# One class for the eight PSUM banks, shared SBUF buffers, and new orders for two stages of a two-layer decoder step

## The chip, the core and the metric

The kernel runs on one core of a Trainium2 chip, as one program. The metric is the device time of one execution in microseconds (us), lower is better. A core has five engines that each work through a list of instructions of their own, in order: TensorE (PE, matrix products; its weight loads are shown apart as PEld), VectorE (DVE), ScalarE (ACT), GpSimd (POOL), and SyncE (SP, which here only issues DMA transfers). Products are written to PSUM, which this kernel cuts into eight banks of 128 x 512 numbers; operands lie in SBUF.

## The reference, cut to what matters

One step of a two-layer decoder for a prompt of 512 tokens and 8 samples of one token each, so 520 columns. Layer 0 is sparse attention with a paged cache, layer 1 is an mLSTM with four heads of width 512.

```python
for i in range(DEPTH):                       # 2 layers, D_MODEL 1024
    hp = rmsnorm(yp, norm_w[i]);  hs = rmsnorm(ys, norm_w[i])
    if i % 2 == 0:
        dp, kvp, wp = nsa_prompt(hp, *prm)
        ds, kvs, wsm = nsa_sample(hs, cache_kv[l], cache_win[l], page_table, *prm)
    else:
        dp, Cp, np_, mp, cp = mlstm_mixer(hp, ...)      # prompt, from a zero state
        ds, Cs, ns_, ms, cs = mlstm_mixer(hs, state_conv[l], state_C[l], state_n[l], state_m[l], ...)
    yp = yp + dp;  ys = ys + ds
y_prompt = rmsnorm(yp, final_norm_w);  y_sample = rmsnorm(ys, final_norm_w)

def nsa_attend(...):          # three branches, each a masked softmax, mixed by gates
    ...
    return gates[..., 0:1] * o_c + gates[..., 1:2] * o_s + gates[..., 2:3] * o_w

def mlstm_mixer(h, conv_buf, C0, n0, m0, chunk, ...):
    proj = h @ w_in;  xm, z = proj[..., :D_INNER], proj[..., D_INNER:]     # D_INNER 2048
    ...                                      # conv of width 4, silu, q, k, v in blocks of 4, gates
    hc, C, n, m = mlstm_cell(...)            # S, num / max(|den|, .), new C and n
    hn = hc * lax.rsqrt(jnp.mean(hc * hc, axis=-1, keepdims=True) + RMS_EPS)
    out = (hn * norm_w + skip * c) * jax.nn.silu(z)
    return out @ w_out, C, n, m, xpad[:, T:]
```

## The kernel before, in words

**Tiling.** Everything is kept transposed: 128 features on the partitions, the 520 tokens along the free axis, in two halves of 260 where a projection is made. A weight is loaded as float32 (`wraw`), rounded to a high part (`whi`, on ACT or DVE) and a low part (`wlo` = raw - hi, on POOL or DVE), and each product is three matmuls, hi by hi, lo by hi, hi by lo. The activations are split in the same way (`hhi`/`hlo` after the norms, `uh`/`ul` before the output projection). A result leaves PSUM on DVE or ACT: `x<-x,mm`, for instance, is DVE adding a finished product to the residual, and it is the last reader of that bank.

**Stages.** `step_kernel` runs through them in this order: (1) norm, k and v projections, and the compression of the cache pages of the samples (0 to about 205 us); (2) the q and z projections (to about 300); (3) attention, prompt tiles and samples interleaved (about 300 to 470); (4) the output projection of layer 0, the `xm` projection and the convolution of layer 1 (to about 650); (5) the z projection with the first states of the samples (to about 757); (6) the heads alone: q, k, v, the scores, the other states and the output projection of the heads that are done (to about 1009); (7) the rest of the output projection, the final norm and the last rows of C.

**What sets the order.** The program is recorded, and then each engine's list is emitted in an order that is written down: five stages as a list of swaps (`MOVED...`), and three as a permutation of the pieces of a plan: `ORDER0` for attention, `ORDER1` for stage 5, `ORDER2` for stage 6, with `MOVEDP0` to `MOVEDP2` naming the pieces that run on another engine than the plan's own. No engine overtakes within its list, so an instruction that waits holds up all that stands behind it.

**PSUM.** `bank(tag, bufs, name)` makes a PSUM tile of one bank. The eight banks form four classes: `mm` with 2 (`mmb()`: projections, values, products with the state), `s` with 3 (`sb()`: scores and sums), `t` with 2 (`xb()`: transposes, short rows, `kwh` products), `d` with 1 (`db()`: the samples' scores and products with the state). A new tile of a class takes the place of the oldest one of that class, and its first matmul waits until the last reader of that older tile is done.

**SBUF.** Buffers form rings by tag in the same way: raw, high and low weights 2 each, `w1h` and `w1l` 3 each, the page splits `phi`/`plo` 2 each, the attention's scores 7 (`SBUFS`) and transposed scores 8 (`PTB`), and one ring for each row of the heads (`wb`, `ctw`, `q`, `kwh`, `kwl`, `cpt`; `wt`, `acc`, `sq1`, `hx`, `hy`).

**Names used later.** `dec_qk` (L1163) makes the scores of the samples against one cache tile `dk` (`d<-dk,QZ`, 8 pages loaded by SP), `d<-dk,dpt` is the product with the values. `s<-KA,qst` and `s<-KB,qst` are the prompt's scores, `s<-cst,s` and `t<-cst,s` its transposes, `mm<-pt,VN` its values. In the heads `s<-q,CT` is the score, `hx`, `hy`, `num` are the rows of a head's normalised output, `ul<-num,uh` and `ul<-HN,uh` the low parts of what goes into the output projection (`mm<-uh,whi`), `cs<-t,wk,cs` a state's update. All instructions go through one helper, so a profile shows nearly all of them at line 504; they are told apart by the names of their tiles.

Of the kernel before, what the change touches and what calls it, by code (L numbers as in the profile page):

```python
# [9 lines left out]
F32 = mybir.dt.float32  # L10
F32R = mybir.dt.float32r
# [33 lines left out]
SBUFS = 7  # L45
PTB = 8
# [7 lines left out]
W3B = (2, 6, 6)  # L54
# [486 lines left out]
def step_kernel(ctx, tc, ap):  # L541
# [19 lines left out]
    def bank(tag, bufs, name=None):  # L561
        return ps.tile([128, 512], F32, name=name or tag, tag=tag, bufs=bufs)
# [6 lines left out]
    def mmb():  # L569
        return bank("mm", 2)  # L570

    def sb():
        return bank("s", 3)

    def xb():
        return bank("t", 2)

    def db():
        return bank("d", 1)
# [2286 lines left out]
```

## Time and profile before

| what | value |
|---|---|
| median of 3 runs | 1055.37 us (1055.33 to 1056.41) |
| the profiled execution | 1052.93 us, of which the span of the core is 1051.2 us |
| busy in that span | PE 1022.5, PEld 909.5, DVE 787.8, ACT 535.0, POOL 393.3 us |
| granted TensorE clock, mean | 0.995 |
| read and written | 145.89 MB and 58.10 MB |

The profiled execution is 2.44 us, or 0.23%, below the median of the runs. The span is the time from the first to the last instruction; 1.7 us of the profiled time lie around it. Busy time of PE is counted from the start of a matmul to its modelled end. Matmuls overlap: one of 260 columns lasts 0.28 us in the trace and the next starts 0.12 us later, so that a start that comes up to 0.16 us late leaves no idle time behind.

### The profile page before, as it was taken

The page shows a single profiled execution, that of the slowest core. Times are in us where ns is not written, and L with a number is a line of the kernel's source. Part 1 is how long each engine was busy: PE and PEld are TensorE (multiplying, and loading weights), DVE is VectorE, ACT ScalarE, POOL GpSimd, SP SyncE. Part 2 cuts the span into 40 slices and gives each one's busy share as a digit, 9 for nine tenths or more (in the row PEclk, how much of TensorE's full clock was granted, in tenths as well). Part 3 has the DMA queues.
Part 4 walks back from the last instruction along what each step waited for, and adds up shares of the span by engine and source line. Part 5 has one row for each costly group of instructions (what it writes and reads, how often), then busy time and mean ns, then how long its engine had stood idle before and what let it go on. Part 6 is the DMA issues. An engine that isn't in the chain of part 4 may idle for free.

```text
span 1051.2 us, 24005 instructions
## 1 busy us (share of the span) xinstructions
PE 1022.5 (97%) x8743; PEld 909.5 (87%) x8743; DVE 787.8 (75%) x1877; ACT 535.0 (51%) x1230; POOL 393.3 (37%) x430
## 2 busy tenths in 40 slices
PE   7999999999999999999999999999899999999998
PEld 6989999899988877779999998898867688787897
DVE  6877764478468887876877675886477998988875
ACT  5253332532467786651444364566555555563533
POOL 1162333434324546462324442342423234434332
PEclk9999999999999999999999999999999999999999
DMA  7664554123435524547435652787789879889543
GB/s 248 202 192 141 156 155 131 36 96 121 144 106 177 141 81 130 153 142 251 142 111 163 203 162 73 243 302 275 259 277 328 273 267 303 295 293 325 161 134 112
DMA packets 124792, 197.19 MB, mean 188 GB/s; under 512 B 16117, under 2 KB 66166, under 8 KB 124418
## 3 DMA queue, kind: packets, MB, share of 16 engines
q1 hardware_dynamic: 118866, 186.37, 54.8%
q10 hardware_dynamic: 5808, 9.28, 2.5%
q8 instruction: 69, 1.13, 0.5%
q14 instruction: 49, 0.40, 0.1%
HBM read 145.89 MB, written 58.10 MB: 194 GB/s over the span
## 4 chain that ended last, share of the span: by engine, by line
PE 83%; DVE 8%; ACT 3%; issue 2%; DMA 1%; SPq 1%; POOL 0%; DVEq 0%; ACTq 0%; POOLq 0%
PE mm L504 51%; PE s L504 18%; PE t L504 10%; PE d L504 5%; ACT s L504 1%; DVE num L504 1%; DVE s L504 1%; DVE cs L504 1%; SPq L504 1%; DMA dk<-in_cache 1%; DVE x L504 1%; DVE qst L504 1%; DMA nw<-in_norms 1%; DVE wlo L504 0%; ACT pt L504 0%
## 5 line engine op out<-in xcount | busy, mean ns | idle before, releaser
L504 PE MATMUL mm<-hhi,whi 128*128 128x260 f32 (+1 forms) x952 | 273.9, 288 | 2.2 <-DVE xm L504 1.3
L504 PE MATMUL mm<-hhi,wlo 128*128 128x260 f32 (+1 forms) x952 | 270.4, 284 | 1.0 <-POOL wlo L504 0.7
L504 PE MATMUL mm<-hlo,whi 128*128 128x260 f32 (+1 forms) x952 | 270.3, 284 | 0.0
L504 PEld LDWEIGHTS mm<-hhi,whi 128*128 128x128 f32 (+1 forms) x952 | 179.2, 188 | 7.2 <-issue 1.7
L504 PEld LDWEIGHTS mm<-hhi,wlo 128*128 128x128 f32 (+1 forms) x952 | 179.1, 188 | 1.6 <-POOL wlo L504 0.9
L504 PEld LDWEIGHTS mm<-hlo,whi 128*128 128x128 f32 (+1 forms) x952 | 178.9, 188 | 0.8 <-DVE hlo L504 0.3
L504 POOL TENSOR_TENSOR wlo<-wraw,whi 128x1024 fp32r<-128x1024 f32 (+2 forms) x55 | 108.8, 1979 | 159.0 <-DVE whi L504 74.8
L504 DVE SCALAR_TENSOR_TENSOR cs<-t,wk,cs 128x512 f32<-128x512 f32 x128 | 88.6, 742 | 6.0 <-ACT cs L504 3.8
L504 ACT ACTIVATE cs<-cs,SBC 128x1024 f32<-128x1024 f32 x64 | 72.0, 1142 | 13.2 <-PE d L504 12.5
L504 POOL TENSOR_SCALAR s<-s,sm 128x128 f32<-128x128 f32 (+3 forms) x63 | 62.8, 1008 | 41.8 <-DVE sm L504 21.1
L504 ACT ACTIVATE s<-s,mn 128x256 f32<-128x256 f32 (+3 forms) x128 | 70.6, 554 | 14.7 <-DVE mn L504 12.7
L504 PE MATMUL s<-phi,w1h 128*128 128x256 f32 (+1 forms) x256 | 77.0, 301 | 0.0
L504 PE MATMUL s<-plo,w1h 128*128 128x256 f32 (+1 forms) x256 | 74.5, 291 | 2.2 <-DVE plo L504 2.0
L504 PE MATMUL s<-phi,w1l 128*128 128x256 f32 (+1 forms) x256 | 74.0, 289 | 0.0
L504 ACT ACTIVATE whi<-wraw 128x1024 fp32r<-128x1024 f32 (+1 forms) x55 | 48.0, 874 | 45.2 <-PE mm L504 34.6
L504 PE MATMUL mm<-uh,whi 128*128 128x260 f32 x224 | 66.5, 297 | 3.6 <-DVE x L504 3.6
L504 DVE CUSTOM_DVE_ANT_0 s<-s,D 128x256 f32<-128x256 f32 (+3 forms) x128 | 57.7, 486 | 10.4 <-PE s L504 7.7
L504 PE MATMUL mm<-uh,wlo 128*128 128x260 f32 x224 | 63.3, 282 | 0.0
L504 PE MATMUL mm<-ul,whi 128*128 128x260 f32 x224 | 63.2, 282 | 0.0
L504 DVE TENSOR_TENSOR wlo<-wraw,whi 128x1024 fp32r<-128x1024 f32 (+1 forms) x47 | 51.9, 1106 | 3.1 <-ACT whi L504 1.8
L504 PEld LDWEIGHTS s<-plo,w1h 128*128 128x128 f32 x256 | 48.5, 189 | 3.9 <-DVE plo L504 2.5
L504 PEld LDWEIGHTS mm<-uh,whi 128*128 128x128 f32 x224 | 42.2, 188 | 9.2 <-DVE x L504 4.5
(479 smaller groups left out, 2650.2 us busy)
## 6 DMA issues: line engine op xcount, KB each, us to landing
cs<-in_state_C SPq DMA_DIRECT2D x64, 512.0 KB, 6.0
o_cs<-cs SPq DMA_DIRECT2D x64, 512.0 KB, 4.8
praw<-in_cache SPq DMA_DIRECT2D x128, 128.0 KB, 3.3
dk<-in_cache SPq DMA_DIRECT2D x128, 128.0 KB, 2.9
wraw<-in_m_in SPq DMA_DIRECT2D x32, 512.0 KB, 4.2
wraw<-in_m_out SPq DMA_DIRECT2D x32, 256.0 KB, 4.4
wraw<-in_w_kv SPq DMA_DIRECT2D x11, 512.0 KB, 4.7
wraw<-in_w_q SPq DMA_DIRECT2D x8, 512.0 KB, 3.6
```

Of the source, the lines that this page charges most:

```text
L504: return f(*[real(x) for x in a], **{n: real(x) for n, x in k.items()})
```

## The change: what it does

1. **One PSUM class.** `bank(name)` takes no class and no number; all tiles have the tag `bank` with 8 buffers. `mmb`, `sb`, `xb` and `db` only differ in the name that the tile gets. In the program as built, a new tile then takes the bank that was given back longest ago in 643 of 663 cases.
2. **Score bank kept per tile.** `dec_qk` kept its bank under `D["dst"]`. It now keeps it under `D["dst", u]`, so that a second tile's product may be started before the first has been read.
3. **Shared SBUF rings.** Raw, high and low weights share one ring of 6, the two halves of `w1` one of 6, `phi` and `plo` one of 4, scores and transposed scores one of 15, `cva` and `cvs` one of 4, the block diagonals one of 7, the rows of the heads one of 9 and one of 6; in stages 6 and 7 the `m_out` weights have one of 6, and at the very end one of 20 with `kwh`, `kwl` and `cpt` (`W3B`). No ring is smaller in sum than its parts were.
4. **Orders stated anew.** `ORDER0` with `MOVEDP0` (attention) and `ORDER2` with `MOVEDP2` (heads alone) are other permutations and other choices of engine. `MOVEDP0` names 121 pieces instead of 131 (72 in both), `MOVEDP2` 106 instead of 100 (47 in both). `ORDER1`, `MOVEDP1` and the `MOVED` lists of the other stages stay, and with them the order of PE in those stages.

```diff
-W3B = (2, 6, 6)
+W3B = (8, 6, 6)
 ORDER0 = (
-    792, 8, 13, 28, 9, 11, 14, 10, 31, 16, 15, 29, 17, 54, 830, 0, 12, 32, 914, 18, 37, 33, 34, 55, 911, 19, 59,
...
+    792, 8, 13, 71, 9, 54, 14, 10, 137, 11, 28, 15, 16, 34, 12, 55, 59, 80, 17, 828, 56, 793, 18, 801, 29, 23,
...
-    def bank(tag, bufs, name=None):
-        return ps.tile([128, 512], F32, name=name or tag, tag=tag, bufs=bufs)
+    def bank(name):
+        return ps.tile([128, 512], F32, name=name, tag="bank", bufs=8)
...
-        return bank("mm", 2)
+        return bank("mm")
...
-        return bank("d", 1)
+        return bank("d")
...
-            D["dst"] = db()
+            D["dst", u] = db()
...
-            V.tensor_add(PS[:, u * 128:(u + 1) * 128], PS[:, u * 128:(u + 1) * 128], D["dst"][:, 0:128])
+            V.tensor_add(PS[:, u * 128:(u + 1) * 128], PS[:, u * 128:(u + 1) * 128], D["dst", u][:, 0:128])
...
-            X["raw"] = wp.tile([128, 8, 128], F32, name="wraw", tag="wraw", bufs=WRAW)
+            X["raw"] = wp.tile([128, 8, 128], F32, name="wraw", tag="w", bufs=WRAW + 4)
...
-            X["hi"] = wp.tile([128, 8, 128], F32R, name="whi", tag="whi", bufs=2)
+            X["hi"] = wp.tile([128, 8, 128], F32R, name="whi", tag="w", bufs=WRAW + 4)
...
-            X["lo"] = wp.tile([128, 8, 128], F32R, name="wlo", tag="wlo", bufs=2)
+            X["lo"] = wp.tile([128, 8, 128], F32R, name="wlo", tag="w", bufs=WRAW + 4)
...
-                X["pt", gk] = at.tile([128, 512], F32, name="pt", tag="pt", bufs=PTB)
+                X["pt", gk] = at.tile([128, 512], F32, name="pt", tag="sp", bufs=SBUFS + PTB)
...
-            X["kwh"] = c2.tile([128, T], F32R, name="kwh", tag="kwh", bufs=1)
+            X["kwh"] = c2.tile([128, T], F32R, name="kwh", tag="row", bufs=9)
...
-            X["x"] = ce.tile([128, T], F32, name="hx", tag="hx")
+            X["x"] = ce.tile([128, T], F32, name="hx", tag="row", bufs=6)
...
-        pk, kh = xb(), fn.tile([128, T], F32R, name="kwh", tag="kwh", bufs=2)
+        pk, kh = xb(), fn.tile([128, T], F32R, name="kwh", tag="w", bufs=20)
```

The built program shows what the new orders move. Three places follow; line numbers in the kernel after are one lower than before.

**SP, early in attention.** `dk<-in_cache` is the load of one of eight pages of a cache tile, `ISA` ahead of it sets its address, `TENSOR_LOAD pt` reads the page numbers of the next tile, and `wraw<-in_w_o` are weights of the output projection, which stage 4 uses. Before, between two of the first tiles of attention (at 312.93 us in the trace):

```order
L504 ISA
L504 DMA dk<-in_cache 128x256
L504 DMA wraw<-in_w_o 128x1024 x2
L777 TENSOR_LOAD pt
L777 ISA x16
L504 ISA
```

and after:

```order
L503 ISA
L503 DMA dk<-in_cache 128x256
L776 TENSOR_LOAD pt
L776 ISA x16
L503 ISA
```

The two weight loads have moved behind later tiles, one by one tile and the other by three.

**PE, at the third and fourth `d<-dk,QZ` of attention.** Before:

```order
L504 MATMUL s<-KB,qst 128x512
L504 MATMUL d<-dk,QZ 32x128 x16
L504 MATMUL s<-KA,qst 128x384
L504 MATMUL s<-KB,qst 128x384
L504 MATMUL s<-cst,s 128x128 x4
L504 MATMUL t<-cst,s 128x128 x4
L504 MATMUL s<-KA,qst 128x384
L504 MATMUL s<-KB,qst 128x384
L504 MATMUL d<-dk,QZ 32x128 x16
```

and after:

```order
L503 MATMUL s<-KB,qst 128x384
L503 MATMUL d<-dk,QZ 32x128 x16
L503 MATMUL s<-KA,qst 128x512
L503 MATMUL s<-KB,qst 128x512
L503 MATMUL s<-KA,qst 128x512
L503 MATMUL s<-KB,qst 128x512
L503 MATMUL s<-KA,qst 128x384
L503 MATMUL s<-KB,qst 128x384
L503 MATMUL t<-KQ,qst 128x64 x8
L503 MATMUL d<-dk,QZ 32x128 x16
```

The transposes `s<-cst,s` and `t<-cst,s` of the first prompt tile now come after the second of these products, with more scores ahead of them.

**DVE, where the third head is finished.** From the products of `hx` to the last `num` rows, before:

```order
L504 TENSOR_TENSOR hx<-hx,hy 128x512 x2
L504 SCALAR_TENSOR_TENSOR hy<-hx,hy 128x512
L504 TENSOR_TENSOR x_13658<-x_13658,mm 128x260
L504 TENSOR_TENSOR x_12742<-x_12742,mm 128x260
L504 TENSOR_TENSOR num<-num,hy 128x512
L504 SCALAR_TENSOR_TENSOR num<-CT_10968,par,num 128x512
L504 TENSOR_TENSOR num<-num,zs 128x512
L504 TENSOR_TENSOR num<-num,hy 128x512
L504 SCALAR_TENSOR_TENSOR num<-CT_10863,par,num 128x512
L504 TENSOR_TENSOR x_12742<-x_12742,mm 128x260
L504 TENSOR_TENSOR x_12729<-x_12729,mm 128x260
L504 TENSOR_TENSOR num<-num,hy 128x512
```

and after:

```order
L503 TENSOR_TENSOR hx<-hx,hy 128x512 x2
L503 SCALAR_TENSOR_TENSOR hy<-hx,hy 128x512
L503 TENSOR_TENSOR wlo<-wraw,whi 128x512
L503 TENSOR_TENSOR num<-num,hy 128x512
L503 SCALAR_TENSOR_TENSOR num<-CT_10968,par,num 128x512
L503 TENSOR_TENSOR num<-num,hy 128x512
L503 SCALAR_TENSOR_TENSOR num<-CT_10863,par,num 128x512
L503 TENSOR_TENSOR num<-num,zs 128x512
L503 TENSOR_TENSOR x_13513<-x_13513,mm 128x260
L503 TENSOR_TENSOR x_13436<-x_13436,mm 128x260 x2
L503 TENSOR_TENSOR num<-num,hy 128x512
```

From the first of these rows to the last `ul<-HN,uh` of the head DVE now has 8 of the additions to `x` instead of 11, the others standing behind, and one `num<-num,zs` more, which POOL did before. In stages 6 and 7 together DVE has four more `wlo`, four more `whi`, three more `num<-num,zs`, and two more each of `ul<-num,uh` and `acc<-acc,sq`; it has three `q` rows and two `cpt` rows less. In attention the shares of the engines stay within 1 us of what they were, by the durations of the trace of before.

More of the change, by code (lines that the diff above doesn't have):

```diff
@@ L615, in load_w @@
         pool, n = pool or wp, bufs or (WRAW, 2, 2)
-        raw = pool.tile([128, kt, f], F32, name="wraw", tag="wraw", bufs=n[0])
+        raw = pool.tile([128, kt, f], F32, name="wraw", tag="w", bufs=sum(n))
         d = q.dma_start(raw, src)
@@ L619, in load_w @@
             last["w"] = d.ins
-        hi = pool.tile([128, kt, f], F32R, name="whi", tag="whi", bufs=n[1])
+        hi = pool.tile([128, kt, f], F32R, name="whi", tag="w", bufs=sum(n))
         S.activation(hi, raw, AF.Copy)
-        lo = pool.tile([128, kt, f], F32R, name="wlo", tag="wlo", bufs=n[2])
+        lo = pool.tile([128, kt, f], F32R, name="wlo", tag="w", bufs=sum(n))
         lo_of(lo, raw, hi, eng)
@@ L708, in step_kernel @@
     xc, wkv = [], {}
-    raw0 = wp.tile([128, 8, 128], F32, name="wraw", tag="wraw", bufs=WRAW)
+    raw0 = wp.tile([128, 8, 128], F32, name="wraw", tag="w", bufs=WRAW + 4)
     for c in range(2):
@@ L719, in step_kernel @@
     S.preload_act_table_set("natural_log_exp_and_others")
-    hi0 = wp.tile([128, 8, 128], F32R, name="whi", tag="whi", bufs=2)
-    lo0 = wp.tile([128, 8, 128], F32R, name="wlo", tag="wlo", bufs=2)
+    hi0 = wp.tile([128, 8, 128], F32R, name="whi", tag="w", bufs=WRAW + 4)
+    lo0 = wp.tile([128, 8, 128], F32R, name="wlo", tag="w", bufs=WRAW + 4)
     for k in range(2):
@@ L1816, in xm_silu @@
         a, ct = conv.pop(ft), CT[ft]
[L1817 removed]
+        s = mi.tile([128, NTOK], F32, name="cvs", tag="cv", bufs=4)
         sigmoid_into(s, a)
@@ L2143, in load @@
         def load():
-            X["raw"] = wp.tile([128, 8, 128], F32, name="wraw", tag="wraw", bufs=WRAW)
+            X["raw"] = wp.tile([128, 8, 128], F32, name="wraw", tag="w", bufs=WRAW + 4)
             SP.dma_start(X["raw"], ap["m_in"][16 + ft])
         def high():
-            X["hi"] = wp.tile([128, 8, 128], F32R, name="whi", tag="whi", bufs=2)
+            X["hi"] = wp.tile([128, 8, 128], F32R, name="whi", tag="w", bufs=WRAW + 4)
             S.activation(X["hi"], X["raw"], AF.Copy)
         def low():
-            X["lo"] = wp.tile([128, 8, 128], F32R, name="wlo", tag="wlo", bufs=2)
+            X["lo"] = wp.tile([128, 8, 128], F32R, name="wlo", tag="w", bufs=WRAW + 4)
             lo_of(X["lo"], X["raw"], X["hi"], E[e])
@@ L2360, in f_bdk @@
         def f_bdk():
-            X["bdk"] = block_diag(c2, wc[:, 1, ft], "bdk", 5)
+            X["bdk"] = block_diag(c2, wc[:, 1, ft], "bdk", 7, "bd")
         def f_bdm():
-            X["bdm"] = block_diag(c2, mw[:, ft], "bdm", 2)
+            X["bdm"] = block_diag(c2, mw[:, ft], "bdm", 7, "bd")
         def f_ctw():
-            X["ctw"] = big("ctw", n=T) if late else c2.tile([128, T], F32, name="ctw", tag="ctw")
+            X["ctw"] = big("ctw", n=T) if late else c2.tile([128, T], F32, name="ctw", tag="row", bufs=9)
             V.tensor_tensor_reduce(X["ctw"], ct, D["wb_", hd], 1.0, 0.0, op0=OP.mult, op1=OP.add,
@@ L2375, in f_q @@
         def f_q():
-            X["q"] = c2.tile([128, T], F32, name="q", tag="q")
+            X["q"] = c2.tile([128, T], F32, name="q", tag="row", bufs=9)
             S.activation(X["q"], X["po"], AF.Copy)
@@ L2407, in f_cpt @@
         def f_cpt():
-            X["cpt"] = c2.tile([128, T], F32, name="cpt", tag="cpt", bufs=2)
+            X["cpt"] = c2.tile([128, T], F32, name="cpt", tag="row", bufs=9)
             S.activation(X["cpt"], X["pc"], AF.Copy)
@@ L2553, in f_y1 @@
         def f_y1():
-            X["y"] = ce.tile([128, T], F32, name="hy", tag="hy")
+            X["y"] = ce.tile([128, T], F32, name="hy", tag="row", bufs=6)
             S.activation(X["y"], X["x"], AF.Ln)
@@ L2645, in load @@
         def load():
-            X["raw"] = fw.tile([128, 4, 128], F32, name="wraw", tag="wraw", bufs=FWB[0])
+            X["raw"] = fw.tile([128, 4, 128], F32, name="wraw", tag="w", bufs=sum(FWB))
             SP.dma_start(X["raw"], ap["m_out"][ft][:, 4 * hd:4 * hd + 4])
         def high():
-            X["hi"] = fw.tile([128, 4, 128], F32R, name="whi", tag="whi", bufs=FWB[1])
+            X["hi"] = fw.tile([128, 4, 128], F32R, name="whi", tag="w", bufs=sum(FWB))
             S.activation(X["hi"], X["raw"], AF.Copy)
         def low():
-            X["lo"] = fw.tile([128, 4, 128], F32R, name="wlo", tag="wlo", bufs=FWB[2])
+            X["lo"] = fw.tile([128, 4, 128], F32R, name="wlo", tag="w", bufs=sum(FWB))
             lo_of(X["lo"], X["raw"], X["hi"], E[e])
@@ L2752, in step_kernel @@
             mm3(pc, kh[:, s_], kl[:, s_], D["vh_", hd, i], D["vl_", hd, i], i == 0, i == 3)
-        cpt = fn.tile([128, T], F32, name="cpt", tag="cpt", bufs=2)
+        cpt = fn.tile([128, T], F32, name="cpt", tag="w", bufs=20)
         S.activation(cpt, pc, AF.Copy)
```

41 lines of the change are left out of this document (20 added, 21 removed), and 191 rows, old and new, of tables (MOVEDP0, MOVEDP2, ORDER0, ORDER2).

## The prediction

> **What bounds the kernel now.** I read the page first, for the engine that is full, then the windows by stage, for where that engine is not, then its waits and, row by row, its timeline. The page's busy times, two rows of its slices and its chain:
>
> ```profile
> PE 1022.5 (97%) x8743; PEld 909.5 (87%) x8743; DVE 787.8 (75%) x1877; ACT 535.0 (51%) x1230; POOL 393.3 (37%) x430
> PE   7999999999999999999999999999899999999998
> DVE  6877764478468887876877675886477998988875
> PE 83%; DVE 8%; ACT 3%; issue 2%; DMA 1%; SPq 1%; POOL 0%; DVEq 0%; ACTq 0%; POOLq 0%
> ```
>
> PE is the bound: 1022.5 of 1051.2 us, and the change removes no matmul. All that it can win is in the other 28.7 us and in starts that come late under a modelled end. The windows by stage say where (time, then busy us of each engine with its instructions, the clock, DMA share, GB/s):
>
> ```profile
> 0.00:200.00 200.00, 191.35 (x1472) 186.79 (x1473) 135.66 (x268) 80.60 (x198) 68.56 (x71) 1.00 0.52 162
> 200.00:300.00 100.00, 97.22 (x869) 94.88 (x872) 66.21 (x147) 40.10 (x94) 32.57 (x26) 0.98 0.34 105
> 300.00:475.00 175.00, 171.83 (x2020) 140.29 (x2013) 140.42 (x537) 125.25 (x387) 90.69 (x103) 1.00 0.47 139
> 475.00:757.00 282.00, 279.63 (x2380) 265.24 (x2381) 200.40 (x389) 138.47 (x292) 100.27 (x120) 0.99 0.59 199
> 757.00:985.00 228.00, 223.68 (x1601) 167.95 (x1591) 196.06 (x424) 128.28 (x211) 81.33 (x90) 0.99 0.85 286
> 985.00:1012.00 27.00, 24.24 (x198) 22.86 (x198) 25.78 (x64) 9.32 (x21) 8.19 (x7) 1.00 0.57 179
> 1012.00:1051.20 39.20, 34.58 (x242) 31.52 (x240) 23.26 (x52) 12.94 (x30) 11.68 (x13) 1.00 0.32 102
> ```
>
> PE's idle time is 8.65, 2.78, 3.17, 2.37, 4.32, 2.76 and 4.62 us from the first row to the last. In the heads (757 to 1012) DVE is the second full engine, 86% and then 95%. What PE waits for, the rows that matter here:
>
> ```profile
> PE s L504 <- ACT sq L504: 5.6, 1, 5.6
> PE mm L504 <- DVE x L504: 3.6, 4, 1.5
> PE t L504 <- DVE pr L504: 2.4, 1, 2.4
> PE d L504 <- DMA dk<-in_cache: 1.5, 3, 0.8
> PE mm L504 <- DVE xm L504: 1.3, 1, 1.3
> PE t L504 <- ACT cpt L504: 0.7, 1, 0.7
> ```
>
> `mm<-DVE x`, `mm<-DVE xm` and `t<-ACT cpt` have an odd look: a projection reads neither `x` nor `xm`, and the next `cpt` product reads no `cpt`. These are waits for a bank, until the engine that empties it has finished. The timeline shows them (start, length, and in brackets the idle time):
>
> ```profile
> 200.99 0.28 PE L504 MATMUL t<-cst,kct 128*32 128x128 f32 x1 [0.46 <-DVE VNEW L504]
> ...
> 308.63 0.39 PE L504 MATMUL s<-KA,qst 128*128 128x512 f32 x1
> 308.87 0.40 PE L504 MATMUL s<-KB,qst 128*128 128x512 f32 x1
> 309.39 0.47 PE L504 MATMUL s<-KA,qst 128*128 128x512 f32 x1
> ...
> 529.54 0.39 PE L504 MATMUL mm<-hhi,whi 128*128 128x260 f32 x1 [1.30 <-DVE xm L504]
> ...
> 1003.25 0.28 PE L504 MATMUL mm<-uh,wlo 128*128 128x260 f32 x1
> 1004.82 0.36 PE L504 MATMUL mm<-uh,whi 128*128 128x260 f32 x1 [1.30 <-DVE x L504]
> ...
> 1041.50 0.51 PE L504 MATMUL t<-vh,kwh 128*128 128x512 f32 x1 [0.69 <-ACT cpt L504]
> ```
>
> At 309.39 no idle time is noted, and yet the start comes 0.52 us after the one before it, where 308.63 to 308.87 is 0.24: 0.28 us lost behind a bank. I went through every first write of a bank and asked whether the bank's last reader had ended less than 0.2 us before. That is so at 72 places, the first and the last being the rows at 200.99 and 1041.50, none before 200. Lateness against the usual spacing sums to 2.2 us in 200 to 300 (6 places), 2.5 in attention (36), 2.7 in 475 to 757 (9), 3.3 in 757 to 985 (16) and 4.4 behind that (5), 15.1 us in all.
>
> **The change, part by part.**
>
> *Single class.* It costs no instruction. Where PE's order stays (stages 1, 2, 4, 5 and 7), I gave the new program's tiles the times of before: the bank taken has then been free for at least 1.29 us, at the median 9.2 us (before: 2.2). So the waits go there, as far as nothing else is late next.
> - 200 to 300: of 2.2 us, most lies at 200.99 to 204.0, where the next matmuls need a sigmoid of ACT that ends at 202.45 in any case. I take 0.7, ends 0 and 2.2.
> - 475 to 757: the row at 529.54 alone is 1.46 us against the usual 0.12, and its operands lie ready. I take 2.3 of 2.7; ends 1.3 and 2.7.
> - 1012 to 1051: two waits of `t`, 0.46 us at 1037.8 and 0.8 at 1041.50 (0.69 in the row, the rest by spacing). Nothing but `cpt` stands there: 1.3, ends 0.7 and 1.3.
>
> *Shared SBUF rings.* A weight load may now follow the last matmul that used an old `whi`, and not the `wlo` that used an old raw part. With the times of before eight loads of stages 4 and 7 start later, the worst by 4.1, 2.6 and 1.7 us. A load lands after
>
> ```profile
> DMA to landing us min/median/max: 3.5/4.3/7.9
> ```
>
> (`wraw`, 560 to 640) and all still land before ACT or DVE take them up; the one that is 2.6 us late is issued at 570.3 and taken up at 581.6. The cover is that slack: 0, ends 0 and 1.5.
>
> *Bank per tile in `dec_qk`.* It only keeps two tiles apart; 0.
>
> *New order of attention.* The 36 waits sum to 2.5 us; I take 2.0, for a few of them have an operand right behind the bank. SP sets the pace of the cache tiles, and the two weight loads ahead of a tile
>
> ```profile
> 312.93 0.84 SPq L504 DMA_DIRECT2D wraw<-in_w_o  x2
> ...
> 403.64 0.64 PE L504 MATMUL d<-dk,dpt 128*32 128x256 f32 x8 [0.78 <-DMA dk<-in_cache]
> ```
>
> go behind later ones; the second wait shown is for a value tile whose buffer is now free 2.7 us of PE work earlier (8.5 against 5.8). The product of one tile early on, though, stands 2.7 us earlier in PE's own work, so its load has less time. I take 0.5 net, ends -1.0 and 1.5. The rows `s<-cst,s` have more PE work between a score and its transpose than before (4.7 against 3.5 us at the tenth percentile), `mm<-pt,VN` a little less (1.48 against 1.58). DVE, ACT and POOL keep their load. Together 2.5, ends -1.0 and 4.0.
>
> *New order of the heads, and what moves to DVE.* The bank waits are 3.3 us in 757 to 985. Against them stands DVE:
>
> ```profile
> L504 DVE TENSOR_TENSOR x<-x,mm 128x260 f32<-128x260 f32 x72 | 29.7, 420 | 22.2 <-PE mm L504 18.3 <-DMA wraw<-in_w_o 3.5
> L504 DVE TENSOR_TENSOR wlo<-wraw,whi 128x512 fp32r<-128x512 f32 x12 | 8.3, 703 | 0.9 <-ACT whi L504 0.7
> L504 DVE CAST whi<-wraw 128x512 fp32r<-128x512 f32 x11 | 5.5, 506 | 8.4 <-DMA wraw<-in_w_kv 6.1 <-DMA wraw<-in_m_out 1.5 <-PE mm L504 0.7
> L504 DVE TENSOR_TENSOR ul<-num,uh 128x512 fp32r<-128x512 f32 x8 | 5.9, 757 | 0.0
> L504 DVE TENSOR_TENSOR num<-num,zs 128x512 f32<-128x512 f32 x7 | 5.3, 752 | 0.1
> L504 DVE TENSOR_TENSOR acc<-acc,sq 128x512 f32<-128x512 f32 x4 | 2.8, 688 | 0.3 <-ACT sq L504 0.3
> L504 DVE COPY q<-mm 128x512 f32<-128x512 f32 x6 | 4.1, 680 | 0.0
> ```
>
> Four `wlo` (2.8), four `whi` (2.0), three `num` (2.3), two `ul` (1.5) and two `acc` (1.4) come, 10.0 us; three `q` and two `cpt` go (3.4); with the small ones the balance is +6.3 us on DVE, and 13 us less on POOL. DVE had 33.2 us of idle time from 757 to 1012, so it fits, but not everywhere without a delay. The work between a score's operand and its product `s<-q,CT` also falls, at the tenth percentile from 3.4 to 2.2 us. The wait for `pr` (2.4 us, at 760.35) is set by the stage before, and stays. I take 1.3, ends -6.3 (all of the new DVE work on the path) and 3.3.
>
> *985 to 1012.* PE stalls there twice, 1.46 us at 997.48 and 1.30 at 1004.82, both behind the additions `x`, which stand behind `num` on DVE. With banks to spare PE runs ahead. But then it needs `ul<-HN,uh`, the end of DVE's own series, at 1011.0. From `hx` to there DVE now has three additions less (3 x 0.42) and one `num<-num,zs` more (0.75), 0.5 us less; summed over all rows from the head's first `hx` row on, its work falls from 24.5 to 23.6 us. I take that 0.9 of the 2.8 that PE stalls; ends 0 and 2.8.
>
> Sum: 0.7 + 2.3 + 1.3 + 0 + 2.5 + 1.3 + 0.9 = 9.0 us. From the profiled execution, 1052.93 us, that is 1043.9; it lies 2.4 us below the median of the runs, so on the scale of the median, 1046.4 us. I say 1046.5. A measurement of this kernel can tell about 0.2%, 2.1 us, from no change.
>
> The Trainium skill has a rule that speaks against a gain: Perfetto Trace Analysis, section Matmul Optimizations, asks that all eight PSUM banks be used. Two, three, two and one were in use already, so by that alone the sum is 0 and the time 1055.4. In the section Optimizing Tensor Performance, Matmuls, it asks that independent groups rotate through different banks so that the next one overlaps the emptying of the last; the rows at 529.54 and 1004.82 are places where two `mm` banks did not do that, and I go by them.
>
> **The rivals.**
> - *All of it, and the clock too.* The granted clock falls to about half three times, each for some 3.4 us; two of them, with the stretch ahead of the second:
>
> ```profile
> 204.40:208.00 3.60, 3.56 (x18) 3.40 (x17) 0.23 (x1) 2.29 (x4) 0.97 (x3) 0.53 0.61 180
> 757.00:760.80 3.80, 1.20 (x44) 0.78 (x33) 2.48 (x12) 1.46 (x5) 2.03 (x5) 1.00 0.85 285
> 760.80:764.40 3.60, 3.48 (x8) 1.56 (x8) 2.88 (x16) 1.21 (x5) 0.00 (x0) 0.53 0.67 153
> ```
>
>  Each costs (1 - 0.53) x 3.6 = 1.7 us, and comes after a stretch with little work on PE. If all 15.1 us of bank waits go and the first dip with them, the time is 1055.4 - 16.8 = 1038.6; the new orders can do as much without the clock, since PE's idle time of 3.17 us in attention and 4.32 in the heads isn't all for banks. Against it: the sigmoid at 202.45, the wait for `pr` and DVE at 95% stay. The Trainium skill (TensorE: Matmul & The Clock Gate, HAM oscillation) ties the fall to idle gaps over about 3.4 us; the longest gap ahead of these falls is the 2.4 us of `pr`, so the trace does not bear that length out. Chance 0.20.
> - *No change.* The waits are replaced by waits for operands right behind them: a bank that is free early only lets PE run into the next late row. For it: at 202.45, at 760.35 and at 1011.0 this is what happens, and PE is 97% busy. Against it: 36 small waits in attention with operands that lie ready, and 529.54. Within 2.1 us of 1055.4, chance 0.11.
> - *Slower: DVE becomes the bound of the heads.* It was 86% busy from 757 to 985 with PE idle for 4.32 us (1.9%), and 95% from 985 to 1012 with PE idle for 2.76 us (10%). If the 6.3 us on DVE make two thirds of the first stretch behave like the second, PE loses 0.083 x 152 = 12.6 us there. The other terms give back 7.7, so the time is 1055.4 - 7.7 + 12.6 = 1060.3. It decides once the heads lose more than 9.8 us (7.7 and the 2.1 of the measurement). Against it: DVE's mean load there comes to 88% or so. Chance 0.14.
> - *As summed*, 1041 to 1053: chance 0.55.
>
> **How the numbers follow.** The sum's own ends, where they do not all fall together, give 1041 to 1053. Down to 1038 the range takes in half of the first rival, up to 1057.5 the no-change case and the nearest part of the slower one: 0.55 + 0.11 + 0.12 + 0.04 is 0.82. Faster by over 0.2%: 0.55 + 0.20 = 0.75; within: 0.11; slower: 0.14.
>
> **What the profile after would show.** Right: `mm<-DVE x`, `mm<-DVE xm` and `t<-ACT cpt` gone or under 0.5 us each in PE's waits; PE idle in attention below 2 us; 475 to 757 shorter by 2 us or more; the stretch after the last head shorter by about 1.3. Wrong: new rows of PE waiting for DVE (`VB`, `q`, `Sl`, `vl`) of several us in the heads, with DVE above 93% there; `wlo` or `wraw` rows among PE's waits in stage 4, where the rings would cost; or a `d` row with more than 1.5 us of `dk<-in_cache` in attention, where the new order would run ahead of SP.

## The result, and the profile after

The changed kernel takes 1046.65 us at the median (1044.04 to 1049.47, 8 runs), the kernel before 1055.35 in the runs beside it: ratio 0.9932, 95% interval 0.9914 to 0.995, or 7.2 us less; the two medians lie 8.7 us apart. One of the eight runs of before took 5627 us, and the ratio leaves it out. Beside the first experiments the changed kernel gave 0.9932 again (0.9909 to 0.9956). The profiled execution took 1046.6 us, its span is 1044.9 us.

The page's busy times and the start of its chain, after:

```profile
PE 1016.1 (97%) x8743; PEld 912.3 (87%) x8743; DVE 793.4 (76%) x1889; ACT 531.4 (51%) x1224; POOL 386.3 (37%) x424
PE 73%; DVE 9%; DMA 6%; ACT 6%; issue 3%; SPq 2%; POOL 1%; DVEq 0%; ACTq 0%; POOLq 0%
```

The span is 6.3 us shorter, and PE's busy time is 6.4 us shorter for the same 8743 matmuls. Its idle time is 28.8 us and was 28.7. So the net gain does not show as idle time: the three rows of waits for a bank named in the prediction, 5.6 us together, are gone, other waits have come in their place, and what is shorter is the busy time, in which late starts had lain under the modelled end of the matmul before. PE's waits after, the rows that matter here:

```profile
PE s L503 <- ACT sq L503: 5.7, 1, 5.7
PE t L503 <- DVE pr L503: 2.3, 1, 2.3
PE mm L503 <- DVE wlo L503: 1.9, 2, 1.6
PE t L503 <- DVE hs L503: 1.4, 1, 1.4
PE d L503 <- DMA dk<-in_cache: 1.3, 1, 1.3
PE mm L503 <- POOL wlo L503: 1.2, 2, 0.7
PE t L503 <- ACT VT L503: 1.0, 1, 1.0
PE d L503 <- DMA cs<-in_state_C: 0.9, 2, 0.7
PE d L503 <- DVE cs L503: 0.9, 1, 0.9
```

`mm<-DVE x`, `mm<-DVE xm` and `t<-ACT cpt` are gone; `t<-DVE hs` and `t<-ACT VT` are new, just behind 200 us. The same instructions that stood behind a bank, in PE's timeline after:

```profile
526.93 0.28 PE L503 MATMUL mm<-hhi,wlo 128*128 128x260 f32 x1
527.05 0.29 PE L503 MATMUL mm<-hhi,whi 128*128 128x260 f32 x1
...
990.57 0.28 PE L503 MATMUL mm<-uh,wlo 128*128 128x260 f32 x1
990.69 0.28 PE L503 MATMUL mm<-uh,whi 128*128 128x260 f32 x1
...
996.87 0.38 PE L503 MATMUL mm<-uh,whi 128*128 128x260 f32 x1 [0.27 <-ACT whi L503]
997.09 0.28 PE L503 MATMUL mm<-ul,whi 128*128 128x260 f32 x1
999.00 0.39 PE L503 MATMUL mm<-uh,wlo 128*128 128x260 f32 x1 [1.63 <-DVE wlo L503]
...
1034.58 0.39 PE L503 MATMUL t<-vh,kwl 128*128 128x512 f32 x1
1034.81 0.39 PE L503 MATMUL t<-vh,kwh 128*128 128x512 f32 x1
```

The start at 527.05 (529.54 before) comes 0.12 us behind its neighbour, that at 1034.81 (1041.50) 0.23. At 996.87 (1004.82) the wait for a bank has become, one product later, a wait for a low part that DVE makes at 998.26.

**Where the time went, stage by stage.** PE runs the same list in the stages whose order stays, and each stage begins with the same matmul in all kernels here. So I took the time between such matmuls. One thing has to be taken off first. The granted clock falls to half for 3.4 us (in four of the profiles one fall lasts 6.8 us), one to five times in an execution, and not always at the same places. The first row is of before, where it fell at 651.6; the other two are of after, which has no fall there and one near 77 us that before has not:

```profile
651.60:655.20 3.60, 3.60 (x38) 1.73 (x41) 1.13 (x8) 0.35 (x2) 0.00 (x0) 0.53 0.86 266
```

```profile
649.00:653.00 4.00, 3.49 (x49) 2.24 (x49) 1.96 (x14) 1.29 (x5) 0.19 (x1) 1.00 0.69 232
75.00:80.00 5.00, 4.62 (x25) 4.62 (x26) 2.28 (x6) 2.55 (x5) 2.54 (x4) 0.67 0.56 192
```

I took off 1.7 us for each fall, (1 - clock) times the stretch. With that taken off each stage, the change against before in us ("to 200" counts from the first matmul; the single class alone, the fixed pages and so on are the experiments below):

```
                        to 200  200-300  attention  475-757  border  heads   end
changed                  +0.1    +0.1     -2.9      -1.6     -0.6    -0.1   -1.5
changed, second profile  +1.0     0.0     -5.4      -1.6     -0.5    -0.2   -2.1
banks alone              +1.7    -0.8     -0.7      -1.9     -0.5    -0.7   -1.1
rings alone              +1.6     0.0     -0.5      +0.2     +0.1    +0.8    0.0
banks and rings          +2.0    -0.4     -1.2      -1.7      0.0    +0.2    0.0
old attention            +0.9    -0.7     -1.7      -1.8     +0.1    +3.2   -1.4
old heads                +2.0    -0.3     -5.2      -2.0     -0.5    -0.1   -1.0
own weight ring          +2.2    -0.4     -4.4      -2.4     -0.4    -0.8   -2.2
end relieved             +1.4    -0.7     -4.2      -2.4     -0.4    -0.7   -1.0
banks, new attention     +4.7    -0.1     -3.8      -2.3     -0.1    -0.2   -0.8
weights later            +1.5    -0.1     +0.9      -2.0     -0.6    -0.6   -0.9
fixed pages              +1.3    -0.1     -2.8      -2.0     -0.4    -0.6   -0.5
own rings                +0.1    -0.2     -4.0      -2.4     -0.4    +7.1   -1.7
```

"Border" is the entry into the heads, "end" what follows the last product of the third head's output.

1.7 us is an upper estimate for a fall of 3.4 us, and not all of them cost it. Where PE runs the same list with and without a fall, the same stretch took 1.6 us longer at 651 and at the border before, 1.1 at the border in the kernels with the single class, about 1.5 at 76, at 205, and in attention at 394 (old order) and 438, and 0.8 at 388 to 394 in the new order of attention; the falls of 6.8 us at 205 cost 2.7. So some gains in the table are too large. In attention it is by 0.9 us for the second profile, old heads, own weight ring and own rings, and by 1.1 for banks with new attention (two falls); between 200 and 300 it is by 0.7 in the lines with -0.7 or -0.8. The attention of "weights later" is too small a loss, since its fall of 6.8 us lies in part in a wait. The border's -0.4 to -0.6 is no gain: the four kernels without a fall there have -0.1 to +0.1.

### The profile page after: what moved, and what is told of

It reads as the page before. It is cut to its first block, busy times and chain, and to the rows that moved or that the text cites. A ratio compares the mean times of both kernels' runs of the same rounds, so it can differ in the third digit from the quotient of the medians.

```text
span 1044.9 us, 24027 instructions
## 1 busy us (share of the span) xinstructions
PE 1016.1 (97%) x8743; PEld 912.3 (87%) x8743; DVE 793.4 (76%) x1889; ACT 531.4 (51%) x1224; POOL 386.3 (37%) x424
## 4 chain that ended last, share of the span: by engine, by line
PE 73%; DVE 9%; DMA 6%; ACT 6%; issue 3%; SPq 2%; POOL 1%; DVEq 0%; ACTq 0%; POOLq 0%
PE mm L503 45%; PE s L503 16%; PE t L503 8%; PE d L503 5%; ACT s L503 3%; DVE cs L503 2%; DMA cs<-in_state_C 2%; SPq L503 1%; DVE num L503 1%; ACT pt L503 1%; DMA praw<-in_cache 1%; DMA wraw<-in_m_in 1%; DMA o_cs<-cs 1%; DMA dk<-in_vwin 1%; DVE qst L503 1%
## 5 line engine op out<-in xcount | busy, mean ns | idle before, releaser
L503 POOL TENSOR_TENSOR wlo<-wraw,whi 128x1024 fp32r<-128x1024 f32 (+2 forms) x51 | 104.1, 2042 | 157.2 <-ACT whi L503 60.4
L503 POOL TENSOR_SCALAR s<-s,sm 128x256 f32<-128x256 f32 (+3 forms) x69 | 70.7, 1034 | 40.7 <-DVE sm L503 30.8
L503 ACT ACTIVATE s<-s,mn 128x384 f32<-128x384 f32 (+3 forms) x128 | 70.6, 554 | 12.0 <-DVE mn L503 10.7
L503 ACT ACTIVATE whi<-wraw 128x1024 fp32r<-128x1024 f32 (+1 forms) x51 | 45.7, 895 | 38.9 <-PE mm L503 19.4
L503 DVE CUSTOM_DVE_ANT_0 s<-s,D 128x384 f32<-128x384 f32 (+3 forms) x128 | 57.4, 486 | 8.7 <-PE s L503 7.7
L503 DVE TENSOR_TENSOR wlo<-wraw,whi 128x1024 fp32r<-128x1024 f32 (+1 forms) x51 | 56.1, 1101 | 4.5 <-ACT whi L503 3.4
L503 PEld LDWEIGHTS s<-phi,w1h 128*128 128x128 f32 x256 | 48.3, 189 | 0.6
```

The source lines that it names most:

```text
L503: return f(*[real(x) for x in a], **{n: real(x) for n, x in k.items()})
```

## The experiments

All twelve were timed in five rounds against the kernel before, four to a chip (1 to 4, 5 to 8 and 9 to 12). Ratios are of paired runs, with their 95% interval; in us they stand against 1054.

**1. The single class alone.** The kernel before with

```diff
-        return ps.tile([128, 512], F32, name=name or tag, tag=tag, bufs=bufs)
+        return ps.tile([128, 512], F32, name=name, tag="bank", bufs=8)
...
-            D["dst"] = db()
+            D["dst", u] = db()
```

> The kernel before with only the single PSUM class of eight banks and the score bank kept per tile; SBUF rings and all orders as before. Theory A (waits for banks are what was paid): the waits of PE for DVE x, DVE xm and ACT cpt vanish with the old orders too; attention about 2 us shorter, 475 to 757 2 us shorter or more, the end 1 to 2 us shorter; in all 5 to 8 us faster than before (ratio 0.992 to 0.995). Rival B (the new orders carry the gain in attention and heads, the banks only the stages whose order stays): attention and heads within 0.7 us of before, in all 2 to 4 us faster (0.996 to 0.998).

Measured: 0.9939 (0.9919 to 0.996), 6.4 us faster. Of the changed kernel's 7.2 us this is most. By time that is theory A; by place it is not quite. From 475 to 757 it gains 1.9 us and at the end 1.1, about as foreseen, but in attention only 0.7 (1.2 and about 1.5 in the profiles of experiments 3 and 5, which have the old order of attention too). PE's waits there, before it was 1.5 us for pages:

```profile
PE d L504 <- DMA dk<-in_cache: 3.4, 3, 1.3
PE mm L504 <- DVE pt L504: 0.4, 1, 0.4
```

and two of the places in its timeline:

```profile
336.62 0.65 PE L504 MATMUL d<-dk,QZ 128*32 128x128 f32 x16 [1.25 <-DMA dk<-in_cache]
...
345.27 0.97 PE L504 MATMUL d<-dk,QZ 128*32 128x128 f32 x28 [1.26 <-DMA dk<-in_cache]
```

The single steps of PE's list, one against one, give 4.2 us of gains in attention and 3.8 us of losses (steps that differ by 0.1 us or so and more); 1.32 and 1.00 of the losses are these two. So a good half of what the banks free in attention is spent waiting for the cache pages.

**2. The shared rings alone.** Tags and sizes of the SBUF rings as changed, four PSUM classes, old orders; the key `D["dst", u]` of the score bank comes with it:

```diff
-        raw = pool.tile([128, kt, f], F32, name="wraw", tag="wraw", bufs=n[0])
+        raw = pool.tile([128, kt, f], F32, name="wraw", tag="w", bufs=sum(n))
...
```

> The kernel before with only the shared SBUF rings; four PSUM classes and all orders as before. Theory A: no gain, and a small cost where a weight load now stands behind PE's last use of an older high part: the wait of PE for POOL wlo near 567 us, 0.7 us in the changed kernel, shows here too; in all 0 to 1.5 us slower. Rival B (the rings free loads and rows and bring part of the gain): 1 to 3 us faster, with PE idle less in the heads.

Measured: 1.0001 (0.9987 to 1.0015). Nothing by themselves, as theory A had it; the wait near 567 us does not show in this profile.

**3. Single class and rings, old orders.**

```diff
 ORDER0, MOVEDP0, ORDER2, MOVEDP2 as before; all else as changed
```

> The changed kernel with the old orders of attention and of the heads (single class and shared rings stay). Theory A: as the single class alone, within 1 us, since the rings bring nothing by themselves: 5 to 8 us faster than before, so the new orders are worth 1 to 3 us. Rival B: 2 to 4 us faster only, so the new orders are worth 4 to 6 us.

Measured: 0.9977 (0.9962 to 0.9992), 2.4 us faster: rival B's time, and not theory A's, which was the single class alone within 1 us. Under the old orders the rings take back 4 us of what the banks give (0.9977 against 0.9939; the two intervals do not overlap). In its profile the end is where it loses most against the single class:

```profile
PE mm L504 <- DVE wlo L504: 2.0, 2, 1.6
PE mm L504 <- POOL wlo L504: 0.9, 1, 0.9
PE mm L504 <- ACT whi L504: 0.3, 1, 0.3
```

(PE's waits from 980 to 1015) where the single class alone has 0.7 and 0.8 us for the first two. Experiment 6 has the same code there, and 0.7 and 0.8 as well, so that the rings alone don't make these waits. Which ring costs what under the old orders stays open.

**4. The changed kernel again.**

> The changed kernel again, on the same chip as the parts. Both theories: 8 to 9 us faster than before (0.992). If the stretches at half clock near 205, 651 and 757 us are chance and not set by the program, this profile shows them at other places or in another number than the first profile of the changed kernel, which had none at 651; if they are set by the program, they stand where they stood.

Measured: 0.9932 (0.9909 to 0.9956). The falls of the clock: the first profile has one each before 200, in 200 to 300 and at the entry to the heads, this one has them in attention, at that entry and at the end. Of the three places of before only that entry has one in both. Over all fourteen profiles the falls mostly keep to a few places: ten have one at 204 to 207, ten at 753 to 761, six at 388 to 394, five at 76 to 77. Which of them an execution has changes, for one program too. Only before has one at 651.

**5. The old order of attention in the changed kernel.**

```diff
 ORDER0, MOVEDP0 as before; all else as changed
```

> The changed kernel with the old order of attention (ORDER0 and MOVEDP0 as before), all else as changed. Theory A (in attention the freed banks only uncover the wait for the cache pages, and it is the new order that takes that wait away): attention 2 us longer than in the changed kernel, the wait of PE for dk pages 2 to 3.5 us there instead of 1.3; in all 6 us faster than before (0.994 to 0.996). Rival B (banks did it): attention as in the changed kernel within 0.7 us, in all 8 to 9 us faster (0.992).

Measured: 0.9956 (0.9938 to 0.9975), 4.6 us faster than before. Theory A: attention gains about 1.5 us here, its fall taken off at 1.5, where the new order has 2.7 to 4.5, and PE's wait for pages is 1.9 us, just under the 2 to 3.5 expected. The heads are 3.2 us longer in this one profile, which I can't explain by their own list, since it is that of the changed kernel; this execution, of 1052.97 us, is the slowest of the kernel's twelve (median 1048.99).

**6. The old order of the heads in the changed kernel.**

```diff
 ORDER2, MOVEDP2 as before; all else as changed
```

> The changed kernel with the old order of the heads (ORDER2 and MOVEDP2 as before), all else as changed. Theory A (the rings cost at the end with the old order, where m_out weights come late, and the new order only takes that back): the heads up to their last product within 0.5 us of the changed kernel, the stretch behind it 2 to 3 us longer with PE waiting for low parts of the weights; in all 4 to 6 us faster than before (0.994 to 0.996). Rival B (the new order of the heads is worth nothing): as the changed kernel, 0.992 to 0.993.

Measured: 0.9919 (0.9897 to 0.9941). Rival B: no slower than the changed kernel. In the profile the heads take what they take in the changed kernel, and the end is 0.5 to 1.1 us longer; in the timing nothing of that is left. The new order of the heads is worth nothing that these runs can tell.

**7. Streamed weights in rings of their own.**

```diff
-            X["raw"] = wp.tile([128, 8, 128], F32, name="wraw", tag="w", bufs=WRAW + 4)
+            X["raw"] = wp.tile([128, 8, 128], F32, name="wraw", tag="wraw", bufs=WRAW)
...
```

> The changed kernel with the streamed weights of stages 1 to 5 in rings of their own again (2 raw, 2 high, 2 low), all else as changed. Theory A (a load that waits for the last use of an old high part comes too late near 565 us): the wait of PE for POOL wlo there, 0.7 us, goes, and nothing else moves; 0.5 to 1 us faster than the changed kernel, that is 0.991 to 0.993 of before. Rival B (the wait is the transfer's own, from the state loads beside it): unchanged, 0.993, the wait stays.

Measured: 0.992 (0.9895 to 0.9945), within the noise of the changed kernel. The wait itself,

```profile
565.33 0.39 PE L503 MATMUL mm<-hhi,wlo 128*128 128x260 f32 x1 [0.51 <-POOL wlo L503]
```

(PE's timeline of the changed kernel) is gone. Over all profiles here the step at this matmul is late by 0.00 in all seven kernels where these rings are apart, and by 0.75, 0.69, 0.38, 0.37, 0.17, 0.00 and 0.00 us in the seven where they are shared. So the shared ring puts this load on the edge, up to 0.75 us. In the first profile of the changed kernel the load of this weight is issued 1.1 us later than with own rings, counted from when the matmul was due, and takes 8.1 us to land instead of 6.9; ACT's `whi` waits 1.27 us for it. How much of the later landing is the ring's and how much the transfer's own isn't told apart.

**8. DVE relieved at the end.** Two low parts and one `num<-num,zs` to POOL:

```diff
-MOVEDP2 = (..., 863, ..., 903, ...)
+MOVEDP2 = (..., 917, ...)
```

> The changed kernel with three pieces moved from DVE to POOL where the last head is finished: two low parts of m_out weights and one num<-num,zs, 2.05 us of DVE work. Theory A (from 980 to 1006 us DVE is the bound, and PE's 1.2 to 1.6 us wait there for a low part is DVE's queue): that wait goes and the last ul<-HN,uh comes 1 to 2 us earlier; 1 to 1.6 us faster than the changed kernel, 0.991 to 0.992 of before. Rival B (PE's own work sets the end there, the wait is covered later): within 0.3 us of the changed kernel, 0.993.

Measured: 0.9933 (0.9907 to 0.9959). Rival B's time, but not its reason. PE's waits from 975 to 1010:

```profile
PE t L499 <- DVE x L499: 1.6, 1, 1.6
PE mm L499 <- POOL wlo L499: 0.9, 1, 0.9
```

The product that waited 1.6 us for a low part on DVE now waits 0.9 us for the same low part on POOL. PE comes to the next place earlier, and there `t<-bdk,ctw` waits for an addition to `x`, which it does not read: a bank again, with all eight in one class, since the additions that empty the others stand behind DVE's rows of the head. DVE's own series sets the end of this stretch, and it has not become shorter: its last `ul<-HN,uh` ends 27.2 us after the start of "end", and 26.8 and 27.5 us in the two profiles of the changed kernel. One row of DVE, and the row of POOL that was at work when it began:

```profile
988.34 1.66 DVE L499 SCALAR_TENSOR_TENSOR num<-CT,par,num 128x512 f32<-128x512 f32 x1
988.08 1.37 POOL L499 TENSOR_TENSOR wlo<-wraw,whi 128x512 fp32r<-128x512 f32 x1 [2.44 <-ACT whi L499]
```

Three such rows of DVE last 1.64 to 1.75 us here, where they last 0.69 to 0.75 with POOL at rest; each begins while POOL makes a low part and ends 0.55 us behind it. That is 2.9 us more on DVE, against the 2.05 taken off it.

**9. Single class and new attention, old heads, no other ring.** The new order of attention needs the ring that scores and transposed scores share, and nothing else:

```diff
-                    X["s", gk] = at.tile([128, 512], F32, name="s", tag="s", bufs=SBUFS)
+                    X["s", gk] = at.tile([128, 512], F32, name="s", tag="sp", bufs=SBUFS + PTB)
...
```

> The kernel before with the single PSUM class, one ring for scores and transposed scores, and the new order of attention; every other ring and the order of the heads as before. Theory A (banks and the order of attention are all that pays; the other rings cost, and the new order of the heads only makes up for them): attention 3 us shorter than before, the heads as with the banks alone, no wait for low parts near 565 us; in all 8 to 10 us faster than before, 0.990 to 0.992, at least as fast as the changed kernel. Rival B (the rings and the heads' new order carry 2 to 3 us together): 5 to 7 us faster, 0.994 to 0.995.

Measured: 0.9939 (0.9921 to 0.9956), 6.4 us faster: less than theory A, and no better than the single class alone. Its profile has attention 3.8 us shorter by the table, 2.7 with the two falls taken off at what they cost, near the 3 of theory A. It loses 4.7 us before 200 us, where PE's list is that of the single class alone, which loses 1.7 there. 2.9 of the difference is one wait for `DVE plo`, 4.9 us instead of 2.0: `phi<-ones`, two columns wide, begins on DVE at 71.24 while POOL is at work and lasts 5.23 us, until POOL has filled `KB`; with the single class alone it lasts 0.15. Whether its other runs lose there too can't be seen from their times, so why the whole is not faster stays open.

**10. Two weight loads out of the pages' way.** The single class alone, and pieces 914 and 911 of `ORDER0`, the two early `w_o` loads, placed behind piece 798:

```diff
-... 32, 914, 18, 37, 33, 34, 55, 911, 19, ...
+... 32, 18, 37, 33, 34, 55, 19, ...
...
+... 798, 914, 911, ...
```

> The single PSUM class alone, as measured first, with the two early w_o weight loads taken from between the cache pages on SP and put behind the seventh tile; nothing else moves. Theory A (the loads of pages on SP set the early attention, and the two weight loads stand in their way): the two waits of PE for dk pages near 336 and 345 us, 1.3 and 1.0 us with the single class alone, shrink by 0.8 us together or more; in all 0.5 to 1.5 us faster than the single class alone. Rival B (the pages' own issue sets it, the weights stood in a gap): the waits within 0.4 us of what they were, the time unchanged, 0.994.

Measured: 0.9985 (0.9971 to 0.9998), 4.8 us slower than the single class alone. The wait for pages did fall, from 3.4 to 0.8 us. But `whi`, which rounds one of these weights, stayed where it was in ACT's list. The wait of ACT from 315 to 350 us and what it held up on PE, ahead of it the product that waited at 336.62 with the single class alone:

```profile
ACT whi L459 <- DMA wraw<-in_w_o: 6.7, 1, 6.7
```

```profile
330.50 1.08 PE L459 MATMUL d<-dk,QZ 128*32 128x128 f32 x32
...
342.15 1.12 PE L459 MATMUL s<-cst,s 128*128 128x128 f32 x4 [5.16 <-ACT pt L459]
```

`pt` stood behind `whi`. The half of theory A on the pages is borne out by the first of the two waits, which is gone at 330.50 with no other wait ahead of it; the second product stands behind the 5.16 us, so that it tells nothing. The forecast of the time was wrong because I moved a transfer without the instruction that waits for it.

**11. Pages from fixed addresses.** The single class alone, and in `pages`, for attention's tiles:

```diff
             def one(i=i):
+                if row:
+                    SP.dma_start(dst(i), ap["cache"][u * 8 + i:u * 8 + i + 1, :, col:col + n].rearrange("o p f -> (o p) f"))
+                    return
```

> The single PSUM class alone, with the attention's cache pages loaded from fixed addresses instead of from the page table, so that SP reads no page numbers and computes no addresses for them (the same bytes in the same transfers; other pages than the reference asks for). Theory A (in attention the freed banks only uncovered the wait for pages, which SP issues at about 1 us each): PE's wait for dk pages falls from 3.4 to under 1 us and attention is 2 to 3.5 us shorter than with the single class alone. Rival B (the buffers of the pages, freed by PE, set it, not the issue): the waits stay over 2 us and attention within 1 us.

Measured: 0.9928 (0.9905 to 0.9951), 7.6 us faster than before with the old orders. PE's wait for pages, and attention's row of the windows, with PE 172.1 us busy in it (before 171.8; 1.00 is the clock):

```profile
PE d L504 <- DMA dk<-in_cache: 0.5, 1, 0.5
```

```profile
300.00:475.00 175.00, 172.09 (x2029) 143.30 (x2028) 140.70 (x538) 124.66 (x385) 89.68 (x102) 1.00 0.47 146
```

Attention is 2.8 us shorter than before, against 0.7 with the single class alone (0.7 to 1.5 over three profiles of the old order). Theory A: what stood behind the banks in attention was SP's issue of the pages, page numbers and addresses above all: with the single class alone 3.2 us lie between the last page of one early tile and the first of the next, and 0.53 us between pages. By time alone the two kernels can't be told apart (0.9928 and 0.9939). SP itself now waits 55.3 us for PE to free page buffers from 296 to 400 us, where it waited 16.7 us with the single class alone.

**12. All weight rings apart, new orders.**

```diff
-            X["raw"] = fw.tile([128, 4, 128], F32, name="wraw", tag="w", bufs=sum(FWB))
+            X["raw"] = fw.tile([128, 4, 128], F32, name="wraw", tag="wraw", bufs=FWB[0])
...
```

with experiment 7's edit.

> The changed kernel with raw, high and low weights of all stages but the very last in rings of their own again; new orders, single class and the other shared rings as changed. Theory A (the shared weight rings cost a little in stage 4 and at the end): 0.5 to 1.5 us faster than the changed kernel, 0.991 to 0.993. Rival B (they cost nothing that can be measured with the new orders): 0.993, within 0.5 us.

Measured: 1.0028 (1.0011 to 1.0044), slower than before, and 10 us slower than the changed kernel; neither theory had that. It is all in the heads, +7.1 us. PE's waits there, 755 to 990:

```profile
PE d L503 <- DMA cs<-in_state_C: 3.5, 4, 1.6
PE t L503 <- DVE pr L503: 2.3, 1, 2.3
PE mm L503 <- DVE cs L503: 1.9, 2, 1.4
PE t L503 <- DVE x L503: 1.1, 1, 1.1
```

Against experiment 7, only the `m_out` rings differ. SP's waits there:

```profile
SPq L503 <- POOL wlo L503: 13.9, 5, 7.4
SPq L503 <- DMA wraw<-in_m_out: 9.0, 3, 4.3
SPq L503 <- DVE Sh L503: 4.9, 1, 4.9
SPq L503 <- PE mm L503: 1.7, 2, 1.2
```

With two raw buffers a load of `m_out` waits on SP until `wlo` has read the older one, and the loads and stores of the states `cs` stand behind it. The first place is the wait of 4.9 us: the load is issued at 790.18, as soon as DVE's `wlo` is done at 790.15 (the name `Sh` is of the row of DVE behind it), where experiment 7 issues it at 785.44 without a wait. The next loads of `cs` follow 4 to 5 us later than there, and PE waits for one of them:

```profile
805.65 0.64 PE L503 MATMUL d<-cs,QZ 128*32 128x512 f32 x4 [1.55 <-DMA cs<-in_state_C]
```

It is the place that counts and not the sum: in the changed kernel (second profile) SP waits 4.4 us for `POOL wlo` in the heads, none for `wraw`, and 24.5 us in 8 pieces for PE's last use of a slot. So the new order of the heads, which gains nothing over the old one with its rings, is written for the shared ring and loses 10 us without it.

No version beat the changed kernel by more than its interval; the nearest (6, 7 and 11, the last with other pages than asked for) lie at 0.9919 to 0.9928.

## Why the prediction was right, point by point

The time, 1046.5 against 1046.65, agrees better than its terms do, and that is luck: by the paired ratio the gain is 7.2 us where the sum had 9.0, and of its terms the banks in attention and the heads brought less than forecast, and the order of attention more. The mechanism, late starts behind a bank that went with the single class, is what experiment 1 shows. Against the stage table (changed kernel, first and second profile):

- *200 to 300*: 0.7 forecast, 0.0 and -0.1 measured. The bank waits of the start of that stretch went, and waits for `hs` (1.4 us) and `VT` (1.0) took nearly all of it, where I had left a third.
- *475 to 757*: 2.3 forecast, 1.6 and 1.6 measured, and 2.4 in the two kernels with streamed weights in rings of their own, so the term of the banks was right, and the shared ring took 0.7 of it. Of it 1.53 is the one start at 529.54. The waits near 652 looked longer than they were, since the clock was at half there.
- *Attention*: 2.5 forecast, 2.9 and 4.5 measured (the second with its fall taken off at 0.8), right in size and wrong in the split. I put 2.0 on the banks and 0.5 on SP's pages. With the old order the banks give 0.7 to 1.5; taken with pages from fixed addresses (experiment 11) they give 2.8; the new order, which has the weight loads behind the tiles, gives 2.7 to 4.5 in seven profiles. The step "SP sets the pace of the cache tiles" was the right one, and its term, 0.5, was too small, as the 2.0 on the banks was too large. What in the new order does it, SP's list or PE's, no run tells apart.
- *Heads*: 1.3 forecast, 0.1 and 0.2 measured. I summed 3.3 us of late starts from "the bank's last reader ended less than 0.2 us before". With the single class alone, where the list is the old one, the steps that come earlier sum to 1.5 us, and 0.7 is left: many of these starts would have been late anyway. In the changed kernel the waits for the states (`cs`, 0.9 and 0.9 us in its list) stand there in place of `x`. The +6.3 us on DVE (+5.6 on the page) cost nothing that shows; POOL's busy time fell by 7.0 us, not by the 13 that I had.
- *End*: 0.9 + 1.3 = 2.2 forecast, 1.5 and 2.1 measured. The tail gave 0.70 to 0.85 instead of 1.3 in every kernel with the single class: both waits went, and four products behind them start 0.1 to 0.2 us later each. That PE would run ahead and then stand before DVE is what 999.00 shows, and experiment 8 again.
- *Rings*: 0 forecast (0 to 1.5). Under the new orders 0 to 0.75 us near 565, where a load did come after ACT was ready for it, which I had ruled out; under the old orders 4 us in the timing, which the sum did not see. They are not a free rename either: without the `m_out` ring the new order of the heads loses 10 us.
- *The clock*: I had every fall cost 1.7 us and come after a stretch with little work on PE. Measured, one costs 0.8 to 1.6 us, and the one at 651.6 came after 3.4 us in which PE was idle for 0.2.
- *The range*: half of the first rival's 0.20 is 0.10, and the sum of the range has 0.12 for it.

Of the four signs that I had named for "right", the bank waits in PE's rows came in full; 475 to 757 came with 1.6 us for 2 (3.3 as the traces have it, 1.7 of it for the fall at 651 that only before has), and the tail with 0.70 to 0.85 for 1.3. "PE idle in attention below 2 us" did not come (4.4 us from 300 to 475, before 3.2), and it was a bad sign to choose: PE's idle time by the page did not change in sum, and the net gain lay under the modelled ends. Of the signs for "wrong", a low part late in stage 4 came, at 0.7 us.

The rule that the Trainium skill gives in Perfetto Trace Analysis, Matmul Optimizations (use all eight banks), was kept before and after, so it did not tell the two apart. What comes nearer is the one on rotating independent groups (Optimizing Tensor Performance, Matmuls). Four classes rotated as well, each through one to three banks; experiment 1 puts 6.4 us on rotating through all eight.

## What to carry to other kernels

A wait of an engine for another whose result it does not read was a wait for a buffer here; with four small classes of PSUM the last reader of a bank was done just ahead of PE's first write at 72 places, and one class for all eight took 6.4 us off a kernel whose PE was 97% busy, with no instruction changed. Then look at what stood behind that wait: here it was the issue of page loads on SP, which decided what the banks were worth in attention. A transfer is moved together with the instruction that waits for it. A written-out order is tried again with each change of the rings: the new order of the heads lost 10 us with other rings, and the old one lost nothing with the shared ones and the new order of attention. Work moved from one engine to another is priced with what the second does to the first: three pieces given to POOL took 2.05 us off DVE, and 2.9 us came back on it.

## What the runs showed of the hardware

**The spread of the runs is in part the clock.** In 23 runs of the kernel before on the chip of experiments 1 to 4, time and mean granted clock correlate at -0.80 (1049.99 us at 0.998, 1055.64 at 0.993); time multiplied by the clock has a standard deviation of 0.91 us instead of 1.31. On the chip of 5 to 8 (17 runs) the correlation is -0.72, and 1.30 us stand instead of 1.88; on that of 9 to 12 (23 runs) it is -0.55, and the product spreads as much as the time (1.57 and 1.55). By the product the medians on the first chip are 1048.3 before and 1038.8 after, a ratio of 0.991.

**The falls of the clock.** They last 3.4 or 6.8 us and cost 0.8 to 2.7 us each. 36 of the 43 in the fourteen profiles begin behind 3.4 us in which PE was idle for 1.4 us or more. The other seven don't: that at 651.6 in before (0.2 us idle) and the six at 388 to 394 (none), for which I have no explanation. The same idle stretch, at 75 us for instance, is followed by a fall in one execution and not in another. The Trainium skill (TensorE: Matmul & The Clock Gate, HAM oscillation) asks for gaps of over about 3.4 us; here shorter ones were enough at times, the longest ahead of most of them 0.9 to 2.4 us, and the place changed from one execution to the next of the same program.

**DVE beside POOL.** Of 280 rows `num<-CT,par,num` and `hy<-hx,hy` on DVE in the fourteen profiles, twelve last 1.64 to 1.89 us and the others 0.69 to 0.77. Eleven of the twelve begin while POOL is at work on `wlo<-wraw,whi` or `vl<-VT,vh`, and end 0.55 us after it is done; beside POOL's `bdk` and `wt` rows the time stays at 0.69 to 0.77.
